# The same block kernel, with the instruction order of the scheduler's other simulation

## The chip, the cores and the metric

The kernel runs on one core of a Trainium2 chip. A core has engines that each work through a queue of their own, in order: PE (TensorE, matrix products; PEld is its weight load, which overlaps the products), DVE (VectorE), ACT (ScalarE), POOL (GpSimd) and SP (SyncE, which here issues the DMA transfers). An instruction starts when it is at the head of its queue and the semaphores that it waits for have been signalled. The metric is the device time of one execution in microseconds (us); less is better.

## The reference, cut to what matters

One decoder block on a sequence of 512 tokens with 1024 channels, in float32:

```python
mod = (silu(c) @ w_ada + b_ada)                       # six vectors: shift, scale, gate, twice
h = rmsnorm(x) * (1 + scale_m) + shift_m
z, xbc, dt_raw, u_pool, gate_logits = split(h @ w_in)
xs, bmat, cmat = split(silu(causal_conv4(xbc)))       # 2048, 4 x 128, 4 x 128 channels
dt = softplus(dt_raw + dt_bias);  a = -exp(a_log)     # 32 heads in 4 groups
y = ssd_chunked_scan(xs * dt, dt * a, bmat, cmat) + d_skip * xs     # chunks of 128 tokens
y_ssd = rmsnorm_per_group(y * silu(z)) @ w_branch_ssd
y_pool = causal_multiscale_pool(u_pool) @ w_branch_pool
x = x + gate_m * ((g_ssd * y_ssd + g_pool * y_pool) @ w_out)        # g_*: sigmoid(gate_logits)
h = rmsnorm(x) * (1 + scale_f) + shift_f
x = x + gate_f * (square(relu(h @ w_up)) @ w_down)    # 4096 inner channels
return rmsnorm(x)
```

In the scan, each chunk has a decay matrix exp(a_cs[l] - a_cs[s]) for l >= s, where a_cs is the cumulative sum of dt * a within the chunk, and a state that is carried from chunk to chunk.

## The kernel before, in words

Everything is kept with channels on the 128 partitions and the 512 tokens along the free axis. A float32 product is made of three products of a reduced-precision format: each operand is split in a high part (a cast on ACT) and a low part (a subtraction on DVE), and `mm3` issues high x high (L155), high x low (L156) and low x high (L157).

A *unit* is 128 output channels of a projection: `load_unit` loads a 128x1024 weight block by DMA (L140), casts its high part on ACT (L145) and makes its low part on DVE (L146); then 8 x 3 matmuls write one of three PSUM banks in rotation. What reads the bank frees it for the unit three later: the convolution (L395 on ACT, then three L397 on DVE), SiLU (L439, L412), a copy or an addition (L459, L461). Where an instruction that frees a bank stands late in its queue, the later unit waits on PE.

The stages are these. An opening, to about 58 us, in a `manual_schedule` block (first projections, L328). The dt chain: softplus by a series of small DVE operations (L355 to L367), cumulative sum as a matmul (L369), copy (L370), transposes (L373), two activations (L374, L375) and two stores to DRAM (L376 `cs_d`, L377 `ecs_d`). Then four groups of the scan. In a group, `prepare` broadcasts rows of `cs_d` from DRAM to all partitions (L494), adds and exponentiates small decay vectors (L496, L497, L498), masks on POOL (L499), exponentiates eight 128x128 blocks (L503) and multiplies by the scores (L504); transposes (L507) and products follow (L533 old state, L541 and L545 new state, L553 diagonal part), the sum (L561, L571, L573), the gate (L575), squares (L576) and their sums on POOL (L577, L578). At a group's end stands the split of the sums of squares (L125, L126), a matmul that adds them over partitions (L590), a logarithm and an exponential (L593, L594) and the scaling (L600). The function `run` writes units of the next projections between the steps of a group, so that PE has work. The modulation vectors come from `ada`: a 512 KB load (L170 `adaT`) and one DVE reduction (L171), also written between.

After the groups follow the pooling branch, the gates as pairs of half-width products with combined operands (`Pair`, splits at L691 and L692, products at L745), the output projection with residual (L933), squares and their sum (L940, L941), the norm's matmul L950 and its activations (L952, L953), and the scaled input of the MLP (L980 to L982). The MLP begins with four plain products at once (`up_first`) and four plain units, whose Relu, square and split (L1040, L1041, L691, L692) free the two banks they rotate over, and goes on in pairs.

The text of the program does not fix the order in the queues. Apart from the opening, the tile scheduler takes the instructions of the program, simulates the engines and puts out the order of each queue; `high_priority` and `issue_after` in the code are hints and constraints for it. The program gives it no table of numbers; how the simulation is made is a parameter of the context, at L1230. ACT keeps one set of function tables loaded at a time, and a table load is put in wherever neighbouring activations in the order belong to different sets.

## Time and profile before

| | before |
|---|---|
| time, 3 runs | 978.68, 978.77, 980.02 us; median 978.77 |
| the profiled execution | 978.15 us, of which the span from first to last instruction is 976.4 |
| busy: PE, DVE, ACT, POOL | 951.4, 689.7, 517.0, 90.8 us |
| mean granted clock of PE | 0.995 |
| DMA | 129.25 MB, 132 GB/s over the span |

PE is busy in 97% of the span, so time is lost wherever PE waits. The view of waits names for each wait of an engine the line that it waited for; the view of windows gives busy time by stretch; the timeline gives the instructions of one engine in order, with the idle time before one and what ended it in brackets. Consecutive instructions of one engine overlap by some 0.1 us in these rows, so spacings are a little shorter than durations.

### The profile page before, as it was taken

The page shows a single profiled execution, that of the slowest core. Times are in us where ns is not written, and L with a number is a line of the kernel's source. Part 1 is how long each engine was busy: PE and PEld are TensorE (multiplying, and loading weights), DVE is VectorE, ACT ScalarE, POOL GpSimd, SP SyncE. Part 2 cuts the span into 40 slices and gives each one's busy share as a digit, 9 for nine tenths or more (in the row PEclk, how much of TensorE's full clock was granted, in tenths as well). Part 3 has the DMA queues.
Part 4 walks back from the last instruction along what each step waited for, and adds up shares of the span by engine and source line. Part 5 has one row for each costly group of instructions (what it writes and reads, how often), then busy time and mean ns, then how long its engine had stood idle before and what let it go on. Part 6 is the DMA issues. An engine that isn't in the chain of part 4 may idle for free.

```text
span 976.4 us, 13664 instructions
## 1 busy us (share of the span) xinstructions
PE 951.4 (97%) x5279; PEld 810.0 (83%) x5279; DVE 689.7 (71%) x1025; ACT 517.0 (53%) x843; POOL 90.8 (9%) x91
## 2 busy tenths in 40 slices
PE   8999999999899999999999999799999999999996
PEld 4877887888688888877888988798899889889986
DVE  7978879776967787998633797785557655765633
ACT  5479978567346642673421554585147226525732
POOL 0102321320212132300000000000000000000000
PEclk9999999999999999999999999899999999999999
DMA  9736345853464344445221278252244125214002
GB/s 358 300 130 188 126 137 162 211 154 107 152 177 137 92 114 130 145 150 162 83 88 42 66 262 276 87 175 65 65 122 139 57 74 183 78 42 145 30 1 87
DMA packets 62339, 129.25 MB, mean 132 GB/s; under 512 B 4737, under 2 KB 29569, under 8 KB 62274
## 3 DMA queue, kind: packets, MB, share of 16 engines
q1 hardware_dynamic: 62272, 128.38, 41.8%
q8 instruction: 41, 0.67, 0.3%
q14 instruction: 24, 0.20, 0.1%
q10 hardware_dynamic: 2, 0.00, 0.0%
HBM read 126.13 MB, written 2.23 MB: 131 GB/s over the span
## 4 chain that ended last, share of the span: by engine, by line
PE 64%; DVE 16%; DMA 8%; ACT 7%; issue 3%; POOL 1%; SPq 0%; DVEq 0%; POOLq 0%; ACTq 0%
PE ps L156 15%; PE ps L157 15%; PE ps L155 15%; PE ps L745 14%; PE ps L328 4%; DMA d<-cs_d 4%; DVE d L146 3%; DVE s L126 2%; ACT d L145 2%; DMA d<-adaT 2%; DVE s L397 1%; DVE d L171 1%; DMA d<-wout 1%; DVE d L692 1%; ACT d L503 1%
## 5 line engine op out<-in xcount | busy, mean ns | idle before, releaser
L155 PE MATMUL ps<-s,d 128*128 128x512 f32 (+1 forms) x1016 | 386.8, 382 | 3.6 <-DVE s L397 2.9
L156 PE MATMUL ps<-s,d 128*128 128x512 f32 (+1 forms) x1016 | 383.4, 378 | 1.6 <-DVE s L126 1.6
L157 PE MATMUL ps<-s,d 128*128 128x512 f32 (+1 forms) x1016 | 383.7, 378 | 0.0
L155 PEld LDWEIGHTS ps<-s,d 128*128 128x128 f32 x1016 | 190.5, 188 | 42.7 <-issue 5.7
L156 PEld LDWEIGHTS ps<-s,d 128*128 128x128 f32 x1016 | 190.9, 188 | 36.7 <-DVE s L126 2.3
L157 PEld LDWEIGHTS ps<-s,d 128*128 128x128 f32 x1016 | 190.7, 188 | 35.7 <-issue 0.2
L146 DVE TENSOR_TENSOR d<-d,d 128x1024 fp32r<-128x1024 f32 x80 | 103.1, 1290 | 50.5 <-ACT d L145 25.6
L745 PE MATMUL ps<-s,d 128*128 128x256 f32 x1080 | 132.2, 280 | 0.0
L745 PEld LDWEIGHTS ps<-s,d 128*128 128x128 f32 x1080 | 129.9, 188 | 0.4
L145 ACT CAST d<-d 128x1024 fp32r<-128x1024 f32 x80 | 83.3, 1044 | 65.3 <-PE ps L157 20.9
L691 ACT CAST d<-d 128x1024 fp32r<-128x1024 f32 x56 | 58.3, 1050 | 99.1 <-PE ps L156 63.5
L692 DVE TENSOR_TENSOR d<-d,d 128x1024 fp32r<-128x1024 f32 x56 | 68.0, 1224 | 39.1 <-ACT d L691 23.3
L1121 DVE SCALAR_TENSOR_TENSOR xs<-ps,mod,xs 128x512 f32<-128x512 f32 x29 | 21.7, 750 | 69.6 <-PE ps L157 69.6
L691 ACT CAST d<-sz 128x1024 fp32r<-128x1024 f32 x32 | 33.6, 1051 | 68.8 <-PE ps L156 48.9
L171 DVE CUSTOM_DVE_ANT_0 d<-d,d,par_t 128x1024 f32<-128x1024 f32 x32 | 42.7, 1335 | 15.3 <-DMA d<-adaT 15.3
L692 DVE TENSOR_TENSOR d<-sz,d 128x1024 fp32r<-128x1024 f32 x32 | 39.2, 1224 | 19.7 <-ACT d L691 18.4
L503 ACT ACTIVATE d<-d,ncs 128x128 f32<-128x128 f32 x128 | 40.5, 391 | 6.7 <-POOL d L499 6.7
L328 PE MATMUL ps<-s,d 128*128 128x512 f32 x168 | 40.1, 392 | 1.9 <-ACT s L316 1.9
L397 DVE SCALAR_TENSOR_TENSOR s<-ps,par_t,s 128x511 f32<-128x511 f32 (+2 forms) x54 | 39.7, 742 | 0.2
L328 PEld LDWEIGHTS ps<-s,d 128*128 128x128 f32 x168 | 31.4, 188 | 9.6 <-ACT s L316 2.4
L125 ACT CAST s<-s 128x512 fp32r<-128x512 f32 x32 | 19.7, 618 | 25.4 <-POOL s L515 20.2
L126 DVE TENSOR_TENSOR s<-s,s 128x512 fp32r<-128x512 f32 x32 | 25.7, 803 | 9.2 <-ACT s L125 9.2
(230 smaller groups left out, 1098.5 us busy)
## 6 DMA issues: line engine op xcount, KB each, us to landing
d<-adaT SPq DMA_DIRECT2D x32, 512.0 KB, 4.1
d<-wx SPq DMA_DIRECT2D x18, 512.0 KB, 3.7
d<-wdn SPq DMA_DIRECT2D x18, 512.0 KB, 4.2
d<-cs_d SPq DMA_DIRECT2D x16, 512.0 KB, 6.2
d<-wbs SPq DMA_DIRECT2D x16, 512.0 KB, 3.8
d<-wz SPq DMA_DIRECT2D x15, 512.0 KB, 4.4
sz<-wdn SPq DMA_DIRECT2D x14, 512.0 KB, 3.8
d<-wup SPq DMA_DIRECT2D x13, 512.0 KB, 4.1
```

Of the source, the lines that this page charges most:

```text
L145: act.copy(hi[:, :w], r[:, a:a + w])
L146: (low or dve).tensor_tensor(lo[:, :w], r[:, a:a + w], hi[:, :w].bitcast(F32), ALU.subtract)
L155: pe.matmul(ps, whi, xhi[:, t0:t1], start=start, stop=False)
L156: pe.matmul(ps, whi, xlo[:, t0:t1], start=False, stop=False)
L157: pe.matmul(ps, wlo, xhi[:, t0:t1], start=False, stop=stop)
L171: dve.tensor_tensor_reduce(r, r, cbc, 1.0, col("b_ada", j), ALU.mult, ALU.add, mod[:, j:j + 1])
L328: pe.matmul(first[u], w[u][i // 2], h[k][i % 2], start=k == 0 and i == 0, stop=k == 7 and i == 2)
L397: dve.scalar_tensor_tensor(t[:, sh:], ps[:, :T - sh], w(3 - sh), t[:, sh:], ALU.mult, ALU.add)
L503: act.activation(m[:, i, :], m[:, i, :], AF.Exp, bias=ncs[:, c, g * HG + i:g * HG + i + 1])
L691: act.copy(dst[0], src)
L692: dve.tensor_tensor(dst[1], src, dst[0].bitcast(F32), ALU.subtract)
L745: pe.matmul(ps, x, y, start=start and m == 0 and i == 0, stop=m == 3 and i == 2, skip_group_check=True)
```

## The change

One argument of the scheduler's context:

```diff
-    with tile.TileContext(nc) as tc:
+    with tile.TileContext(nc, schedule_with_timeline_sim=True) as tc:
```

With it the scheduler makes its order with another simulation of the engines, one that follows the queues in time. The instructions of the block are the same, on the same engines and of the same sizes; activation-table loads fall from 40 to 29 because ACT's order is another, and the semaphore waits follow the order. Of PE's 5,000 instructions most stand elsewhere in the first 250 us (between a third and all of those in each 50 us from 50 us on, by up to some 150 places) and from 500 us on; from 250 to 450 us the order is nearly the old one. The opening is not moved.

Three places, as the prediction uses them. The first is DVE's queue at the end of the dt chain. `ncs` is the cumulative sum, `dec_80` a decay vector made from a broadcast, `s_100`, `s_103`, `s_150` and `s_163` are convolution tiles. Before:

```order
L366 SCALAR_TENSOR_TENSOR dtk<-s_90_514,dtk 128x128
L397 SCALAR_TENSOR_TENSOR s_100_570<-s_92_550,par_t,s_100_570 128x510
L367 TENSOR_TENSOR s_90_514<-dtk,ea 128x128
L397 SCALAR_TENSOR_TENSOR s_100_570<-s_92_550,par_t,s_100_570 128x509
L370 COPY ncs<-ps_31_178 128x128
L397 SCALAR_TENSOR_TENSOR s_103_578<-s_93_551,par_t,s_103_578 128x511
```

And in the change:

```order
L397 SCALAR_TENSOR_TENSOR s_140_803<-ps_139_778,par_t,s_140_803 128x509
L370 COPY ncs<-ps_31_178 128x128
L509 TENSOR_TENSOR s_154_894<-ps_153_889,dtk 128x512
L146 TENSOR_TENSOR d_191_1104<-d_189_1101,d_190_1103 128x1024
L146 TENSOR_TENSOR d_200_1168<-d_198_1165,d_199_1167 128x1024
L397 SCALAR_TENSOR_TENSOR s_150_864<-ps_149_839,par_t,s_150_864 128x511
L497 TENSOR_TENSOR dec_80<-d_124_712,ncs 128x8
L397 SCALAR_TENSOR_TENSOR s_163_934<-ps_162_909,par_t,s_163_934 128x511
L397 SCALAR_TENSOR_TENSOR s_150_864<-ps_149_839,par_t,s_150_864 128x510
L497 TENSOR_TENSOR dec_80<-d_130_742,ncs 128x8
L397 SCALAR_TENSOR_TENSOR s_163_934<-ps_162_909,par_t,s_163_934 128x510
L397 SCALAR_TENSOR_TENSOR s_150_864<-ps_149_839,par_t,s_150_864 128x509
```

The copy L370 stood among the convolutions of the first tiles; now it stands behind all of them and behind s_140's, and the two L497 that depend on it stand between the L397 of s_150 and s_163. In the order before, all L497 of this group stand behind the first convolutions and ahead of those of s_140.

The second is ACT's queue ahead of the first group's norm (L125 of `s_208`, whose result L590 multiplies). `sz_97` is the gated output of the group. Before:

```order
L576 ACTIVATE s_187_1087<-sz_97_561 128x512
L395 ACTIVATE s_193_1132<-ps_192_1107,par_t 128x512
L503 ACTIVATE d_244_1410<-d_244_1410,ncs 128x128 x8
L496 ACTIVATE cd_79<-d_268_1542 128x8
L576 ACTIVATE s_196_1151<-sz_97_561 128x512
L145 CAST d_239_1375<-d_238_1373 128x1024
L125 CAST s_208_1236<-s_123_711 128x512
```

And in the change:

```order
L576 ACTIVATE s_187_1087<-sz_97_561 128x512
L498 ACT_TABLE_LOAD
L498 ACTIVATE dec_81<-dec_81 128x8
L145 CAST d_261_1505<-d_260_1503 128x1024
L439 ACT_TABLE_LOAD
L439 ACTIVATE sz_178_1031<-ps_214_1251 128x512
L503 ACT_TABLE_LOAD
L503 ACTIVATE d_268_1542<-d_268_1542,ncs 128x128
L480 CAST s_227_1329<-ps_229_1331 128x384
L503 ACTIVATE d_268_1542<-d_268_1542,ncs 128x128
L576 ACTIVATE s_196_1151<-sz_97_561 128x512
L503 ACTIVATE d_268_1542<-d_268_1542,ncs 128x128 x6
```

The L125 of s_208 is the next row behind these. The work of the next group and its table loads now stand between the last squares and ahead of L125; further up, three more table loads stand between the square of s_168 and that of s_187.

The third is ACT's queue at the start of the MLP. `d_1064` is the high part of a weight block, `ps_1022` and `ps_1027` are banks of plain units. Before:

```order
L1040 ACTIVATE pad_1017_5828<-ps_978_5572 128x512
L1040 ACTIVATE pad_1018_5833<-ps_980_5574 128x512
L1041 ACTIVATE pad_1017_5828<-pad_1017_5828 128x512
L1041 ACTIVATE pad_1018_5833<-pad_1018_5833 128x512
L691 CAST s_1003_5804<-pad_1017_5828 128x512
L691 CAST s_1005_5806<-pad_1018_5833 128x512
L691 CAST pad_1089_6281<-pad_1082_6261 128x512
L1040 ACTIVATE pad_1023_5869<-ps_1022_5844 128x512
L691 CAST pad_1103_6361<-pad_1096_6341 128x512
L691 CAST d_1064_6104<-d_1063_6102 128x1024
L1041 ACTIVATE pad_1023_5869<-pad_1023_5869 128x512
```

And in the change:

```order
L691 CAST d_1064_6104<-d_1063_6102 128x1024
L1040 ACTIVATE pad_1017_5828<-ps_978_5572 128x512
L691 CAST pad_1103_6361<-pad_1096_6341 128x512
L1040 ACTIVATE pad_1018_5833<-ps_980_5574 128x512
L1041 ACTIVATE pad_1017_5828<-pad_1017_5828 128x512
L1041 ACTIVATE pad_1018_5833<-pad_1018_5833 128x512
L691 CAST s_1003_5804<-pad_1017_5828 128x512
L691 CAST s_1005_5806<-pad_1018_5833 128x512
L1040 ACTIVATE pad_1023_5869<-ps_1022_5844 128x512
```

The cast of d_1064 stood behind the Relu of ps_978, ps_980 and ps_1022; now it stands ahead of all three.

## The prediction

> **What bounds the kernel now.** I read the page first (engine shares), then PE's waits, then stretches of the places where the order changes, then the chain that ended last and the timelines there.
>
> ```profile
> span 976.4 us, 13664 instructions
> PE 951.4 (97%) x5279; PEld 810.0 (83%) x5279; DVE 689.7 (71%) x1025; ACT 517.0 (53%) x843; POOL 90.8 (9%) x91
> ```
>
> PE is busy 951.4 of 976.4 us, so every other engine together costs 25.0 us. An order that keeps PE's instructions can win 25 us at most; it can lose much more. Which waits make up the 25 us:
>
> ```profile
> PE ps L950 <- DVE sz L941: 5.1, 1, 5.1
> PE ps L156 <- DVE s L126: 3.1, 3, 1.5
> PE ps L155 <- DVE s L397: 2.9, 2, 2.5
> PE ps L328 <- ACT s L316: 1.9, 1, 1.9
> ```
>
> The one at L328 lies in the manually ordered opening, which the change leaves alone. Most of the rest is the start and the end of the program. Now the stretches (columns: length, PE, PEld, DVE, ACT, POOL busy, granted clock, DMA share, GB/s):
>
> ```profile
> 50.00:100.00 50.00, 49.23 (x242) 38.60 (x241) 39.83 (x68) 42.75 (x73) 8.36 (x8) 1.00 0.55 166
> 100.00:150.00 50.00, 50.00 (x271) 41.24 (x270) 40.84 (x65) 41.55 (x78) 14.40 (x14) 1.00 0.43 137
> 250.00:300.00 50.00, 47.10 (x265) 37.97 (x264) 38.95 (x63) 21.99 (x43) 10.62 (x12) 1.00 0.51 154
> 600.00:650.00 50.00, 44.93 (x351) 44.15 (x350) 39.20 (x83) 30.05 (x55) 0.00 (x0) 0.93 0.44 145
> 612.40:617.50 5.10, 0.05 (x1) 0.05 (x1) 4.03 (x7) 1.77 (x3) 0.00 (x0) 0.73 0.49 145
> 617.50:627.00 9.50, 9.50 (x62) 9.32 (x63) 7.27 (x19) 4.72 (x11) 0.00 (x0) 0.78 0.09 34
> ```
>
> From 50 to 150 us PE has 99.2 of 100 us of work, while DVE (39.8 and 40.8 of 50) and ACT (42.8 and 41.6) are busy some 80% and more. That stage has three almost full queues and little slack: it stays hidden behind PE only where each instruction comes in time. The last two rows show what an idle PE costs besides: after the 5.1-us wait the granted clock is below full, (1-0.73)x2x5.1 + (1-0.78)x2x9.5 = 6.9 us at half speed, of which 4.2 us under work. Half of that, 2.1 us, is lost on top.
>
> **The change part by part.** The instructions are the same, but for 11 activation-table loads fewer on ACT (40 to 29). That saving is work of an engine that is 47% idle; I price it at nothing for itself and count it inside the chains. All the rest is order. I followed the new queues by hand with the durations of the trace and list where PE would run into an operand that is not ready. Each term is (time of the longer chain) minus (time of PE's own work between the same two points).
>
> *A, the dt chain, +4.0.* The cumulative sum's copy L370 falls from between L397s of the first convolutions to behind them all. From the last L397 on, the masks depend on it: copy, transposes L373, L374, table load, L375, store to DRAM, broadcast L494, L497.
>
> ```profile
> 70.54 0.29 DVE L370 COPY ncs<-ps 128x128 f32<-128x128 f32 x1
> 71.41 1.22 DVE L146 TENSOR_TENSOR d<-d,d 128x1024 fp32r<-128x1024 f32 x1
> 80.75 0.74 DVE L397 SCALAR_TENSOR_TENSOR s<-s,par_t,s 128x509 f32<-128x509 f32 x1
> 82.99 0.17 DVE L497 TENSOR_TENSOR dec<-d,ncs 128x8 f32<-128x8 f32 x1 [1.42 <-DMA d<-cs_d]
> 85.23 0.17 DVE L497 TENSOR_TENSOR dec<-d,ncs 128x8 f32<-128x8 f32 x1 [2.08 <-DMA d<-cs_d]
> ...
> 26.59 4.78 PE ps L328 x21
> 74.75 6.42 DMA d<-cs_d
> ```
>
> Before, the second L497 comes 82.99-70.54 = 12.45 us after the copy, and only other work of DVE's own, already finished, stands near. Now an L397 of s_150, which must free the bank that the unit ps_182 takes, is queued behind two L497, and behind ps_182 all of PE is queued. Taking 0.4 off for transposes that start at the copy's end, the chain from the transposes is 12.05 + 0.17 + 2x0.66 (L397's spacing) = 13.5 us. PE's work between transposes and ps_182 is 36 matmuls of 4.78/21 = 0.228, 8.2, and 1.1 of small ones: 9.3. The difference is 4.2; I take 4.0. Bounds: 0 (a broadcast that lands 4 us earlier) and 6.2 (the third L497, which came 2.24 us after the second).
>
> *C, the first norm sum L590, +7.5.* It waits for ACT's L125 of s_208.
>
> ```profile
> L503 ACT ACT_TABLE_LOAD x8 | 10.3, 1283 | 0.1
> L576 ACT ACTIVATE s<-sz 128x512 f32<-128x512 f32 x16 | 10.1, 630 | 28.5 <-DVE sz L575 23.1 <-DVE pad L625 5.1
> L412 ACT ACTIVATE xs<-s 128x512 f32<-128x512 f32 x16 | 9.3, 624 | 0.0
> L439 ACT ACTIVATE sz<-ps 128x512 f32<-128x512 f32 x15 | 8.9, 595 | 0.1
> ...
> 125.75 2.45 ACT L503 ACTIVATE d<-d,ncs 128x128 f32<-128x128 f32 x8
> 136.80 1.04 ACT L145 CAST d<-d 128x1024 fp32r<-128x1024 f32 x1
> 132.57 0.62 ACT L125 CAST s<-s 128x512 fp32r<-128x512 f32 x1 [1.31 <-POOL s L578]
> ...
> 130.39 0.74 POOL L577 TENSOR_TENSOR s<-s 128x256 f32<-128x256 f32 x1 [3.16 <-ACT s L576]
> 131.22 1.32 POOL L578 TENSOR_TENSOR s<-s 128x128 f32<-128x128 f32 x1
> 130.62 1.60 DVE L171 CUSTOM_DVE_ANT_0 d<-d,d,par_t 128x1024 f32<-128x1024 f32 x1 [0.32 <-DMA d<-adaT]
> 126.13 4.47 DMA d<-adaT
> ```
>
> Between the exponent of dec_81 (L498) and the last square (L576) ACT's new queue holds six table loads (6 x 1.28 = 7.7), eight and two L503 (3.2), two casts (2.1), four 512-wide activations and one square (3.1) and small ones (1.3): 17.4, less some 0.7 of overlap, 16.7. POOL adds 2.1 and L125 0.6. In front of that L498 stand, on DVE, two ada reductions L171, each behind its adaT transfer (4.47): from the first one's landing to L497 1.6 + 1.3 + five L397 or L575-like of 0.66 + L146 1.2 + L561 1.1, about 9; the landing itself is some 9 us after L533 of ps_164. Sum from that L533: 9 + 9 + 16.7 + 2.1 + 0.6 = 37.5 to 38. PE has from there to L590 103 matmuls (23.5) and 7 of the SSD's small ones: 30.4. Difference 7.5. Bounds: 0 and 11 (the two transfers as slow as the broadcasts below).
>
> *E, F, G, second group, +3.8, +2.4, +2.3.*
>
> ```profile
> 162.49 6.15 DMA d<-cs_d
> 168.77 1.79 POOL d L499
> 184.43 8.02 DMA d<-cs_d
> ```
>
> On SP an adaT load whose slot must first be freed by DVE's L171 now stands ahead of the mask broadcast; then come 6.15 (landing), 1.79 (POOL), three L503 and a copy of 0.58, 9.5 in all, while PE has 25 matmuls (5.7) from the broadcast's issue to ps_279, which needs that copy's bank: 3.8. F is the same for ps_285 behind the 8.02-us broadcast; G is the state sum L545 behind two POOL masks. Bounds 0 and 14 for the three.
>
> *M, the start of the MLP, +5.7.* ACT's cast d_1064 moves ahead of the Relu of the first four products. It overwrites a buffer that PE reads in the last matmul of the unit ps_1027, and ps_1032, next on PE, waits for the Relu of ps_1022, behind it.
>
> ```profile
> 658.70 1.14 ACT L691 CAST s<-pad 128x512 fp32r<-128x512 f32 x2
> 659.73 0.63 ACT L691 CAST pad<-pad 128x512 fp32r<-128x512 f32 x1
> 660.25 0.60 ACT L1040 ACTIVATE pad<-ps 128x512 f32<-128x512 f32 x1
> 661.25 1.07 ACT L691 CAST d<-d 128x1024 fp32r<-128x1024 f32 x1
> ```
>
> While ACT works this off, PE has nothing: 1.07 for the cast, then seven 512-wide activations and casts at 0.5 each (two Relu, one weight part, two squares, two casts), and 0.60 for the last Relu: 5.2 to 5.7. The chain needs no transfer, so it is the surest term; bounds 4 and 7.
>
> *L, the removed wait, -5.1 and -2.1 of half clock.* L950 stands 21 matmuls (0.12 each, 2.5 us) later on PE, and SP issues the two wup blocks that hold DVE up two places earlier:
>
> ```profile
> 600.50 0.33 SPq L1019 DMA_DIRECT2D d<-wup  x1
> 604.14 0.33 SPq L1019 DMA_DIRECT2D d<-wup  x1
> ```
>
> 3.64 us earlier there and 2.5 us here exceed the wait of 5.1; bounds -2.5 and -7.2.
>
> *Small ones.* Six places where one or two instructions stand ahead of the one that frees PE's operand (first units, ps_164, the second L590, two in the MLP, the tail), each from 0.6 (a 512-wide activation) to 1.7 (one with a table load): +8.0 together, bounds 0 and 11. Of the old waits at L126, L397 and the 550 to 600 stretch, 2.0 go.
>
> *Q, half clock after the new waits, +6.* Each at 2.1, as above. The trace has a wait of 5.1 that brought it and one of 2.5 (within the 250 to 300 stretch, at clock 1.00) that did not. C and M are above 5.1; A and E lie between. I count three of the four: 6. Bounds 0 and 8.4.
>
> [...]
>
> Sum: 4.0 + 7.5 + 8.5 + 5.7 + 8.0 - 2.0 - 7.2 + 6 = 30.5 us. On the profiled execution, 978.15 us with 1.7 around its span, that is 1008.7; it lies 0.6 under the median of 978.77, so I say **1009 us**.
>
> **The rivals.** *Faster.* The new order fills PE's waits and the new chains do not decide, since broadcasts and adaT land early and ACT has 11 loads (14 us) less to do. Then up to 5.1 + 2.1 + 2.9 + 3.1 of the old waits go: 965. For it speaks that each term but M contains a transfer; against it that the broadcasts took 6.15 to 8.02 us. It decides only if the second L497 follows the transposes within PE's 9.3 us, and if M is wrong too. *No change.* Only A and M cost (9.7) and L and the lesser waits give it back (9.2): 979. It needs C to G hidden, that is ACT's queue of 16.7 us done in 10. *Slower, but less.* Waits that follow each other are not additive: what PE loses in A lets ACT and DVE catch up for C. With C, E, F and G at half, and Q at 4.2: 4.0 + 3.8 + 4.2 + 5.7 + 8.0 - 2.0 - 7.2 + 4.2 = 20.7, or 999. *Much slower.* The first stage becomes bound by DVE and ACT, each new broadcast queues as the 8.02-us one did, and every term is at its upper bound: 6.2 + 11 + 14 + 7 + 11 + 8.4 - 2.0 - 7.2 = 48, about 1027. *The order does not come out as listed*, because the device's queues sort it: I see no mechanism, since each engine's queue is in order.
>
> **How the numbers follow.** A difference below 0.2% (2 us) can't be told from none here. Forecast around 1009 (1003 to 1017): 0.45. Slower but less, 981 to 1003: 0.27. Much slower, above 1017: 0.16. No change: 0.05, faster: 0.07. The range from 987 to 1027 leaves out the last two cases, a part of the lesser loss and a little above. Chances: faster 0.07, same 0.05, slower 0.88.
>
> **What would show it.** In PE's waits: ps_182's L155 on DVE L397 near 4, L590 on ACT L125 near 7.5, L155 on ACT L459 twice, L155 on ACT L1040 of 5 to 6, and no L950 on L941. PE busy stays at 951 plus 2 per wait with half clock, and its clock row dips at the first and sixth of these, not at 615 us. ACT busy falls by 14. If PE's idle time stays near 25, the chains were wrong; if it grows in places that I do not list, the sum was right by luck.

## The result, and the profile after

| | before | the change |
|---|---|---|
| median (lowest to highest) | 979.39 us, 4 runs (978.68 to 980.11) | 1018.81 us, 4 runs (1016.29 to 1023.15) |
| the profiled execution, and its span | 978.15, 976.4 | 1016.84, 1015.1 |
| mean granted clock of PE | 0.995 | 0.981 |

The change is slower: the ratio is 1.0407, with a 95% interval from 1.0365 to 1.0449. The profiled executions differ by 38.7 us, and the page's first lines split them. They give busy time, share of the span and instructions of each engine:

```profile
span 1015.1 us, 13698 instructions
PE 964.2 (95%) x5279; PEld 814.9 (80%) x5279; DVE 690.9 (68%) x1025; ACT 518.5 (51%) x844; POOL 89.2 (9%) x91
```

PE's 5279 instructions are the same and take 12.8 us longer (964.2 against 951.4). PE's idle time has grown from 25.0 to 50.9, by 25.9. The view of waits of the change's PE says what the idle time waited for (in total, times, the longest):

```profile
PE ps L590 <- ACT s L125: 7.7, 2, 5.9
PE ps L155 <- ACT pad L1040: 6.7, 1, 6.7
PE ps L155 <- ACT s L459: 3.8, 2, 3.2
PE ps L155 <- DVE s L397: 3.7, 2, 3.6
PE ps L533 <- DVE s L545: 2.9, 1, 2.9
PE ps L155 <- ACT s L125: 2.1, 1, 2.1
PE ps L155 <- ACT s L691: 2.0, 2, 1.0
...
PE ps L155 <- ACT s L653: 1.8, 1, 1.8
PE ps L950 <- ACT s L1100: 1.7, 1, 1.7
PE ps L155 <- DVE s L461: 1.5, 1, 1.5
PE ps L156 <- DVE s L126: 1.3, 2, 1.1
```

Before, one wait stood out, L950 on L941 with 5.1. It is gone, and five others of 2.9 to 6.7 us, each at another place, have come, with some ten of 0.8 to 2.1. Most of the 12.8 us of extra busy time are the clock: in the stretches with a granted clock of 0.50 PE has 24.9 us of work in the change and 4.2 before, and by estimate half of the difference, some 10.3 us, is lost (behind the wait of 5.9 matmuls of L155 to L157 follow each other at 0.43 us, and ahead of it, at full clock, at 0.23). Of these 1.7 belong to a stretch at 14.8 us in the opening, which the change doesn't move. The other 2.5 us are busy time at full clock. Stretches of the change around two of the waits (length, PE busy, and so on as before; the number after POOL is the granted clock):

```profile
154.40:160.90 6.50, 0.64 (x3) 0.19 (x1) 2.44 (x4) 6.46 (x15) 1.18 (x2) 0.79 0.52 161
160.90:166.00 5.10, 5.06 (x14) 4.02 (x15) 5.08 (x5) 5.02 (x6) 0.00 (x0) 0.60 0.00 0
686.50:693.40 6.90, 0.26 (x2) 0.00 (x0) 5.21 (x9) 5.32 (x9) 0.00 (x0) 0.80 0.66 215
693.40:698.00 4.60, 4.58 (x12) 3.63 (x13) 1.93 (x3) 2.88 (x5) 0.00 (x0) 0.56 0.02 4
```

In the first row ACT is busy for 6.46 of 6.50 us while PE has nothing to do; behind each wait PE works at a clock of about 0.6, 12 to 14 matmuls in the time of some 20 at a spacing of 0.23 us.

Where in the program the time is lost is seen by comparing when PE has issued the same number of instructions. The change is later by 6 us at 100 us of the kernel before, 13 at 150, 21 at 200, 24 at 250, and still 24 at 300; by 31 at 460 and 32 at 600; by 25 at 622 (the wait at L950 is not there any more); by 34 at 665, and by 36 to 38 from 800 on. So 24 us are lost in the first two groups of the scan, 8 from the third group to 600 us, 9 at the start of the MLP and some 4 behind it, and 7 are won at L950.

### The profile page after: what moved, and what is told of

Same layout as the page of the kernel before. It is cut to its first block, busy times and chain, and to the rows that moved or that the text cites. A ratio compares the mean times of both kernels' runs of the same rounds, so it can differ in the third digit from the quotient of the medians.

```text
span 1015.1 us, 13698 instructions
## 1 busy us (share of the span) xinstructions
PE 964.2 (95%) x5279; PEld 814.9 (80%) x5279; DVE 690.9 (68%) x1025; ACT 518.5 (51%) x844; POOL 89.2 (9%) x91
## 4 chain that ended last, share of the span: by engine, by line
PE 74%; DVE 10%; DMA 6%; ACT 5%; issue 4%; POOL 1%; SPq 0%; DVEq 0%; POOLq 0%; ACTq 0%
PE ps L155 18%; PE ps L156 18%; PE ps L157 18%; PE ps L745 13%; PE ps L328 4%; DMA d<-cs_d 3%; PE ps L553 1%; DVE d L146 1%; DVE d L692 1%; DVE pad L635 1%; DMA d<-wout 1%; ACT d L503 1%; DVE d L171 1%; DVE s L126 1%; PE ps L533 1%
## 5 line engine op out<-in xcount | busy, mean ns | idle before, releaser
L155 PE MATMUL ps<-s,d 128*128 128x512 f32 (+1 forms) x1016 | 387.2, 387 | 24.5 <-ACT pad L1040 6.7
L157 PE MATMUL ps<-s,d 128*128 128x512 f32 (+1 forms) x1016 | 384.7, 381 | 0.0
L155 PEld LDWEIGHTS ps<-s,d 128*128 128x128 f32 x1016 | 191.7, 190 | 66.2 <-ACT pad L1040 7.1
L157 PEld LDWEIGHTS ps<-s,d 128*128 128x128 f32 x1016 | 192.2, 189 | 36.4 <-issue 0.3
L145 ACT CAST d<-d 128x1024 fp32r<-128x1024 f32 x80 | 83.6, 1046 | 101.5 <-PE ps L156 41.3
L146 DVE TENSOR_TENSOR d<-d,d 128x1024 fp32r<-128x1024 f32 x80 | 99.4, 1242 | 47.2 <-ACT d L145 21.2
L692 DVE TENSOR_TENSOR d<-d,d 128x1024 fp32r<-128x1024 f32 x56 | 68.0, 1223 | 39.8 <-ACT d L691 23.9
L692 DVE TENSOR_TENSOR d<-sz,d 128x1024 fp32r<-128x1024 f32 x32 | 39.1, 1224 | 22.8 <-ACT d L691 21.6
L328 PE MATMUL ps<-s,d 128*128 128x512 f32 x168 | 41.5, 402 | 1.9 <-ACT s L316 1.9
L328 PEld LDWEIGHTS ps<-s,d 128*128 128x128 f32 x168 | 32.6, 195 | 10.0 <-ACT s L316 2.4
L397 DVE SCALAR_TENSOR_TENSOR s<-ps,par_t,s 128x511 f32<-128x511 f32 (+2 forms) x54 | 39.4, 740 | 0.4 <-ACT s L395 0.2
L126 DVE TENSOR_TENSOR s<-s,s 128x512 fp32r<-128x512 f32 x32 | 25.8, 805 | 11.7 <-ACT s L125 11.4
L692 DVE TENSOR_TENSOR s<-pad,s 128x512 fp32r<-128x512 f32 x38 | 25.8, 686 | 10.5 <-ACT s L691 10.4
```

What stands on the lines that cost most here:

```text
L145: act.copy(hi[:, :w], r[:, a:a + w])
L146: (low or dve).tensor_tensor(lo[:, :w], r[:, a:a + w], hi[:, :w].bitcast(F32), ALU.subtract)
L155: pe.matmul(ps, whi, xhi[:, t0:t1], start=start, stop=False)
L157: pe.matmul(ps, wlo, xhi[:, t0:t1], start=False, stop=stop)
L328: pe.matmul(first[u], w[u][i // 2], h[k][i % 2], start=k == 0 and i == 0, stop=k == 7 and i == 2)
L397: dve.scalar_tensor_tensor(t[:, sh:], ps[:, :T - sh], w(3 - sh), t[:, sh:], ALU.mult, ALU.add)
```

## The experiments

All of them are the changed kernel with one added function, which chains each engine's instructions in a given order and adds no wait that the data don't ask for:

```diff
+def pin(tc, nc):
+    """Chain the instructions of each engine in the order of ORDER (issue order only, no waits)."""
...
+            tc.add_manual_dep(traced[b], a, info, reason="order")
...
         block_kernel(tc, out=out, **args)
+        pin(tc, nc)
```

ORDER is a list of instructions for each engine: the change's, the one before, or a join of both, cut at a time of the profile of before ("to 90 us": on each engine, what has started by then). So each run computes the whole block, and only the places in the queues differ. Ratios are against the kernel before on the same chip.

**The method itself.** ORDER is the change's own, with nothing moved.

> The changed kernel's own order, fixed by the same edges that the other runs use: 1016 to 1023 us, the same waits within 0.5 us each. It shows that fixing the order costs nothing, and gives a second profile of the same order. In the first profile half clock followed waits of 1.9, 2.1, 2.9, 3.2, 3.6, 5.9 and 6.7 us, but not waits of 1.5, 1.7, 1.8 and 1.8; the half-clock stretches begin and end on a grid of 3.41 us. If the clock falls when PE was idle for more than about 1.85 us of one interval of that grid, waits of 2 to 3.5 us get half clock in one profile and not in the other, by where the grid lies, while 5.9 and 6.7 get it in both; the times differ by 1.7 us for each.

It took 1021.10 us (1016.56 to 1023.94), ratio 1.0435 (1.0398 to 1.0472), against 1.0407 of the change. The same waits stand at the same places within some 0.6 us, but for L155 on L461, which is 2.9 instead of 1.5. What follows: fixing the order in this way changes the time by no more than the runs differ among themselves, and differences of 2 or 3 us between runs of this kind don't say much. That the order, and nothing else of the argument, makes the loss is shown by the run with before's order but for one stretch ("The part that gains"): it keeps the argument and takes 975.39 us.

**C, the first norm sum.** The two last squares are moved ahead of the table loads and L125 ahead of the next group's masks, on ACT (and its split's second half L126 on DVE ahead of an L146):

```diff
 L496 ACTIVATE cd_79<-d_268_1542 128x8
+L576 ACTIVATE s_187_1087<-sz_97_561 128x512
+L576 ACTIVATE s_196_1151<-sz_97_561 128x512
 L412 ACT_TABLE_LOAD
...
 L145 CAST d_261_1505<-d_260_1503 128x1024
+L125 CAST s_208_1236<-s_123_711 128x512
 L439 ACT_TABLE_LOAD
...
-L576 ACTIVATE s_196_1151<-sz_97_561 128x512
-L503 ACTIVATE d_268_1542<-d_268_1542,ncs 128x128 x6
-L125 CAST s_208_1236<-s_123_711 128x512
+L503 ACTIVATE d_268_1542<-d_268_1542,ncs 128x128 x7
```

> The order of the changed kernel, every queue fixed by issue-order edges, with five instructions moved at the first group's end: on ACT the squares L576 of s_187 and s_196 go ahead to behind L496 of d_268, the split L125 of s_208 to behind the cast L145 of d_261; on DVE L126 of s_209 goes ahead of L146 of d_262. The wait of L590 (5.9 us, and 2.0 us of half clock under work behind it) has nothing to wait for then. Theory A (each wait has its own price, as in my sum): 5.9 + 2.0 less, 1018.8 - 7.9 = 1011 us, and the waits behind it stay as they are. Theory B (in the first two groups ACT and DVE are behind, and a wait taken from one place comes back at the next instruction of PE that needs them): L590's wait falls below 1 us, but within the next 15 us of PE's work a new wait on L125 or L126 of the second group appears, or the 3.2 us at L459 grows, and the time falls by less than 3 us.

It took 1016.83 us (1015.55 to 1020.47), ratio 1.0386 (1.0354 to 1.0419): 2 us less than the change, inside both intervals. The wait of 5.9 at L590 is gone. In its place PE waits twice further on, as the timeline of this run shows, first PE's rows, then ACT's:

```profile
171.12 0.79 PE L155 MATMUL ps<-s,s 128*128 128x512 f32 x1 [4.49 <-ACT s L125]
176.76 0.79 PE L156 MATMUL ps<-s,s 128*128 128x512 f32 x1 [1.79 <-DVE s L126]
```

```profile
165.02 1.28 ACT L593 ACT_TABLE_LOAD   x1
...
167.02 1.28 ACT L594 ACT_TABLE_LOAD   x1
...
170.46 0.60 ACT L125 CAST s<-s 128x512 fp32r<-128x512 f32 x1
```

The work that L125 of s_208 was moved past (a SiLU and the masks, each with a table load) now runs behind it; then come the two loads for the norm, and the L125 of the next group that PE needs comes behind all of this. In this run ACT works from 142.68 to 173.15 without a gap. ACT is the limit of this stretch, so this edit in its queue chose which instruction of PE waits, and hardly how long PE waits in all (49.2 us idle in this run's profile, 50.9 in the change's).

**A, the dt chain.** First it is undone: the order of before to 90 us, the change's from there on.

```diff
-ORDER: the change's
+ORDER: before's to 90 us, then the change's for all that is left
```

> Every queue has the order of the kernel before for what starts there in its first 90 us (the whole dt chain, the first masks and all that stands between), and the order of the changed kernel for all the rest. Theory A: the waits of the first 90 us go, 1.0 at L385, 3.6 at L397 and 1.7 of half clock: about 6 us less, 1013 us, and L590 waits 6 to 7 us as before. Rival: the late dt chain, which leaves ACT idle for some 12 us between 88 and 102 us, is the root of all waits up to 210 us; then nearly all of the 24 us of that stage come back, 995 to 1000 us.

It took 1012.62 us (1012.33 to 1016.56), ratio 1.0347 (1.0316 to 1.0377), 6.2 less than the change. The waits at L397 (3.6) and L385 (1.2) are gone, those of the groups stand nearly as they were: L590 5.2, L459 3.6, and L461 even 3.0. What A's own waits and one stretch of half clock cost (3.6 + 1.2 + 1.7 = 6.5) is about what came back. So the late dt chain is not the root of the 24 us of the first groups; that rival falls. Then the opposite, A alone: the change's order to 102 us (its own time) and before's from there on.

```diff
-ORDER: the change's
+ORDER: the change's to 102 us, then before's for all that is left
```

> The change's order until 102 us (the dt chain late, the new first units) and before's order from there on. Undoing this part in the change took 6.2 us. Theory that each part has a price of its own, which can be added: 977 + 6 = 983, between 980 and 986. Rival, that the price depends on the order around it: before's groups have their broadcasts and convolutions placed for an early dt chain, so they meet a chain that is some 15 us late with several waits of 2 to 5 us between 100 and 130 us, and half clock after them: 994 to 1000.

It took 992.97 us (989.67 to 993.87), ratio 1.0145 (1.012 to 1.017): 14 us for the part whose removal gave 6. That is far from the sum (980 to 986) and just under the rival's range (994 to 1000). The waits of PE in this run, and then its chain of work that ended last at the first of them:

```profile
PE ps L156 <- DVE s L126: 6.6, 5, 3.1
PE ps L155 <- ACT s L125: 5.2, 2, 4.8
```

```profile
97.30 6.02 DMA d<-cs_d
...
104.83 2.44 ACT d L503 x8
107.27 0.51 ACT s L125
```

In before's order the eight masks and the splits of the first chunk stand directly behind the broadcast, for a chain that is early; when the broadcast comes late (landing at 103.32 here), they all wait for it, and PE behind them. The change's order has other work there. A part of an order has no price of its own here: the late chain costs 6 in the order made with it, and 14 in the one made without it. The waits lie right behind the join at 102 us, and no other cut was tried, so how much of the 14 belongs to this one join is not shown.

**M, the start of the MLP.** First the cast of d_1064 (and its DVE half L692) is put back behind the Relu of ps_1022, as my theory had it:

```diff
-L691 CAST d_1064_6104<-d_1063_6102 128x1024
 L1040 ACTIVATE pad_1017_5828<-ps_978_5572 128x512
...
 L1040 ACTIVATE pad_1023_5869<-ps_1022_5844 128x512
+L691 CAST d_1064_6104<-d_1063_6102 128x1024
```

> The order of the changed kernel, with the cast L691 of d_1064 (and its DVE half L692) moved back to behind the Relu L1040 of ps_1022, as the kernel before has it; the cast of pad_1103, which waits for a wup transfer, stays between the Relus of ps_978 and ps_980. If the cast makes the wait of 6.7 us before ps_1032, as I forecast, some 5 us of it and 2 us of half clock go: 1012 us. If the transfer behind pad_1103 decides, since everything behind it on ACT can't start before it lands, the wait shrinks by less than 1.5 us: 1017 to 1019 us.

It took 1021.76 us (1018.2 to 1022.38), ratio 1.0423 (1.0386 to 1.0459): nothing won, and the wait for L1040 is 6.9. My theory of M falls. The second run moves the cast of pad_1103 as well, which stands two rows further on:

```diff
-L691 CAST d_1064_6104<-d_1063_6102 128x1024
...
-L691 CAST pad_1103_6361<-pad_1096_6341 128x512
...
 L1040 ACTIVATE pad_1023_5869<-ps_1022_5844 128x512
+L691 CAST pad_1103_6361<-pad_1096_6341 128x512
+L691 CAST d_1064_6104<-d_1063_6102 128x1024
```

> As in the run with the cast moved back, and the cast L691 of pad_1103 (with its L692) moved back behind the same Relu too. Both stand as before; the Relus start when PE's products are done. The wait before ps_1032 falls from 6.7 to 2 to 3.7 us, by the five 0.5-us activations that still stand between the Relu of ps_978 and that of ps_1022, and the time by 3 to 6 us: 1013 to 1016 us. If even then 5 us or more are left, the cause lies ahead of these rows, in ACT's queue before the Relu of ps_978.

It took 1014.94 us (1013.38 to 1016.39), ratio 1.0361 (1.0333 to 1.0388), 3.9 less than the change, and the wait is 3.5, both as expected. The intervals of the two ratios overlap a little; the fall of the wait is the clearer sign. The third puts the whole start of the MLP in before's order, on all engines and the transfers too:

```diff
-ORDER: the change's
+ORDER: the change's to 660 us (its own time), before's to 680 (before's time), then the change's
```

> The change's order, but with before's between 660 and 680 us of before's time: the whole start of the MLP on all engines, the transfers' issues too. Moving the cast and the split of d_1064 alone took nothing, moving pad_1103's cast as well took 3.5. Theory that the start waits for ACT's queue ahead of the Relu of ps_1022, part of it held by a transfer: all of the wait goes, 6.7, and with it the half clock of 1.7: against the change 8 less, 1010, between 1007 and 1013. Rival, that the start is late because ACT and DVE come late out of the stage ahead: a wait of over 2 stays and the time is 1014 to 1018.

It took 1014.03 us (1011.25 to 1017.16), ratio 1.0367 (1.0339 to 1.0395), 4.8 less than the change by the medians and 3.9 by the ratios. A wait of 2.6 stays, so the rival, which gave 1014 to 1018, is right. The chain of this run at that wait:

```profile
679.94 1.19 DVE d L692
...
681.15 5.82 DMA d<-wdn
...
687.05 1.05 ACT d L691
...
691.55 0.61 ACT pad L1040
```

The weight load started at 681.15, when DVE's L692 (679.94 to 681.13) had freed its buffer. So 4.1 of the 6.7 us go with the order at the start of the MLP, and 2.6 stay, in this chain because DVE and the transfers come late out of the stage ahead. Why they are late there was not followed further.

**The halves.** Before's order to 253 us and then the change's; the change's to 277 us (its own time) and then before's:

```diff
-ORDER: the change's
+ORDER: before's to 253 us, then the change's
```

> Every queue has the order of the kernel before for what starts there in its first 253 us (opening, dt chain, the first group and most of the second), and the order of the changed kernel for all the rest. If the losses of the two parts are independent, this takes away the 24.2 us by which the changed kernel is late when it has issued the same number of products: 1018.8 - 24.2 = 994.6 us, 991 to 998. If the later part's waits come from lateness of the first part's, clearly less than 991; if the seam adds waits of its own, above 998.

```diff
-ORDER: the change's
+ORDER: the change's to 277 us, then before's
```

> The counterpart: every queue has the changed order for what starts there in its first 277 us, and the order of the kernel before for all the rest. Independent parts: 979.4 + 24.2 = 1003.6 us, 1000 to 1007, with the 5.1-us wait of L950 back. The two halves' differences to the kernel before add up to that of the whole change, 39.4, within 4 us.

The first took 1001.74 us (999.81 to 1007.54), ratio 1.0251 (1.0213 to 1.0289), 24.6 us over before; the second 998.73 (997.18 to 999.63), ratio 1.0205 (1.017 to 1.0241), 21.6 over. Together that is 46, more than the change's 39.4, so both forecasts were missed: the first run is above its 991 to 998, the second a little below its 1000 to 1007, with 3.6 us and not 5.1 at L950. The first run has a wait of 5.56 us right at its join, on an L397, where the kernel before has 2.48. Whether that belongs to the join was tried with a later cut:

```diff
-ORDER: before's to 253 us, then the change's
+ORDER: before's to 300 us, then the change's
```

> Before's order until 300 us of the block and the change's after that; the earlier run of this kind joined the two orders at 253 us and had a wait of 5.6 us and half clock right at the join. Theory that this wait belongs to the join: the wait near 261 is again 2.5 or less, and the rest costs what the change is later behind 300 us, about 15 (L1040 6.7, the second L590 1.8, L125 2.1, two L691 1.0, half clock 3.4 less the 5.1 of L950): 993, between 990 and 996. Rival, that the change's second half costs more once the first is on time (its 24.6 of that run): 1000 to 1003.

It took 995.49 us (994.44 to 996.43), ratio 1.018 (1.0155 to 1.0206), 16.4 us over before by the medians and 17.6 by the ratio, and the wait on L397 is 2.4 again. With it the halves add up to 21.6 + 16.4 = 38 of 39.4 us. Neither of the two runs has the change's order between 253 and 300 us of before, but there the change loses nothing (24 us late at 250 and at 300). So a little over half of the loss comes from the first 277 us, and what stands behind 300 us costs about the same whether or not the first part is late: some 15 us in the change, 16 to 18 here. The wait at the start of the MLP, too, is 6.3 us in this run.

**The part that gains.** Before's order, and the change's only between before's 540 and the change's 643 us, where L950 stands:

```diff
-ORDER: the change's
+ORDER: before's to 540 us, the change's to 643 (its own time), then before's
```

> The kernel before, except that between its 540 us (last gates) and the end of the output projection (623 us there, 643 us in the changed kernel) every queue has the changed order: the one place in which I forecast that the change wins. There L950 stands 21 products later and two wup blocks are issued two places earlier. If that order wins by itself, the wait of 5.1 us and 2.1 us of half clock go, and waits of some 1 to 2 us come in place of 1.4 us: 979.4 - 7.2 + 1 = 973 us, faster than both. If the wait went away in the changed kernel only because its DVE had caught up in the longer run, L950 waits here too and the time is 977 to 981.

It took 975.39 us (973.32 to 977.50, 12 runs) against 977.16 (17 runs), ratio 0.9978 (0.9961 to 0.9994). The wait at L950 is gone, and with it the half clock of the kernel before at 615 us, so this order does win by itself; some small waits have come (1.9 on L145, 1.0 on L777). This run's profile has half clock at 16.89 and at 262.65 instead (the section on the hardware comes back to both). So 1.8 us came of a wait of 5.1, less than the 6 of the forecast. Then single instructions were moved at the waits that were left, of which DVE's two largest are shown (the others are in the expectation):

```diff
+L397 SCALAR_TENSOR_TENSOR s_398_2270<-ps_397_2245,par_t,s_398_2270 128x511
+L397 SCALAR_TENSOR_TENSOR s_398_2270<-ps_397_2245,par_t,s_398_2270 128x510
+L397 SCALAR_TENSOR_TENSOR s_398_2270<-ps_397_2245,par_t,s_398_2270 128x509
 L146 TENSOR_TENSOR d_436_2481<-d_434_2478,d_435_2480 128x1024
...
+L126 TENSOR_TENSOR s_689_3806<-sz_464_2672,s_688_3805 128x512
+L600 SCALAR_TENSOR_TENSOR sz_464_2672<-sz_464_2672,par_t,s_687_3801 128x512
 L146 TENSOR_TENSOR d_725_4003<-d_723_4000,d_724_4002 128x1024
```

> The order of the splice (before's order, with the change's order only from before's 540 us to the change's 643 us), and five moves at the waits that are left: on DVE the three L397 of s_398 ahead of the weight split L146 of d_436 (the wait of 2.5 us at 261), L126 of s_237 ahead of L146 of d_284 (1.7 us at 160), L126 of s_689 and the fourth L600 ahead of L146 of d_725, on ACT L125 of s_694 ahead of an L846 (together some 2 us at 440), L692 of d_880 ahead of an L881 (0.6 us). Theory that single waits can be taken out where the instruction moved past is not needed by PE soon: the waits at 261, 160 and 440 fall from 2.4 + 1.7 + 2 to under 1.5 together, and no half clock after 261: 970, between 967 and 973. Rival, that each such move only hands the wait to the instruction that it is moved ahead of, as in the run at the group's end: the waits reappear within 20 us, 975 as the splice, plus or minus 1.5.

It took 975.80 us (973.98 to 978.24, 12 runs) against 979.06 (17 runs), ratio 0.9976 (0.9962 to 0.9989): as the run without the moves. Waits of PE, of the run without them and then of the run with them:

```profile
PE ps L156 <- DVE s L126: 3.8, 3, 1.7
PE ps L155 <- DVE s L397: 2.4, 1, 2.4
```

```profile
PE ps L156 <- DVE s L126: 3.4, 4, 1.4
PE ps L155 <- DVE s L397: 2.6, 4, 1.3
...
PE ps L590 <- DVE s L126: 1.0, 1, 1.0
```

One wait of 2.4 on L397 has become four with 2.6 together, and L590 waits 1.0 where it did not; PE is idle for 22.5 us in all, where it was 22.1. The rival of this run is right: the waits are handed on. Both joined orders are faster than the kernel before by 0.2%, each on a chip of its own, with an interval that ends below 1.

## Why the prediction was right or wrong

The time, 1018.8, lies in the range (987 to 1027) and on the side that had 0.88, but 10 us above the number and just above the likeliest case's own range (1003 to 1017). By its time it falls into "much slower" (above 1017, 0.16), and that case's first sentence, that the first stage becomes bound by ACT and DVE, fits what C's run shows of ACT; its sum of all upper bounds (48) did not come. On the profiled execution the sum said +30.5, and +38.7 came. Of the 30.5, 26.6 were waits and 3.9 half clock (6 for the new waits, less 2.1 for L950's). Measured are 25.9 of waits, some 10.3 of half clock and 2.5 of busy time at full clock. So the step that failed by its size is **Q**: it counts three waits that pay, and six did, for 10.7 us in place of 6, besides the 1.7 in the opening. It went by the trace's wait of 2.5, which did not pay, and that of 5.1, which did; here waits of 2.1 to 3.6 paid as well. That the total of the waits agrees so closely is in part luck, by the prediction's own sign: some 7 us of waits stand at places that it does not list (L125 at 468 us, L653, L461, L777, L145), and C, E and F are smaller than said by 4.

| term | predicted | measured |
|---|---|---|
| A, ps_182 on L397 | 4.0 | 3.6 |
| C, the first L590 on L125 | 7.5 | 5.9 |
| E and F, L155 on L459 | 6.2 | 3.8 |
| G, L533 on L545 | 2.3 | 2.9 |
| M, L155 on L1040 | 5.7 | 6.7 |
| L, L950 on L941 | -5.1 | -5.1 |
| old waits on L126, L397 | -2.0 | -4.6 |
| small ones (the rest) | 8.0 | 12.7 |
| half clock | 3.9 | 10.3 |
| busy time at full clock | 0 | 2.5 |

**A** came as worked out. The chain of work that ended last, of the change:

```profile
93.10 0.45 PE ps L373 x4
...
96.92 6.74 DMA d<-cs_d
103.67 0.60 DVE dec L497
104.27 1.32 DVE s L397 x2
105.73 0.47 PE ps L155
```

From the transposes to PE it takes 12.6 us, where 13.5 was said, and the broadcast is again more than half of it.

**C** has its mechanism and nearly its size. ACT's rows of the change, the table loads between the squares among them:

```profile
141.44 0.21 ACT L498 ACTIVATE dec<-dec 128x8 f32<-128x8 f32 x1 [1.48 <-DVE dec L497]
...
151.38 1.28 ACT L498 ACT_TABLE_LOAD   x1
...
153.84 1.28 ACT L439 ACT_TABLE_LOAD   x1
...
155.75 1.28 ACT L503 ACT_TABLE_LOAD   x1
...
158.01 0.62 ACT L576 ACTIVATE s<-sz 128x512 f32<-128x512 f32 x1
...
160.28 0.60 ACT L125 CAST s<-s 128x512 fp32r<-128x512 f32 x1
```

From L498 to the end of the last square ACT works for 17.2 us without a gap (16.7 was said), then come POOL, masks on ACT and L125 to 160.88. How the 1.6 us that are missing divide over the part ahead of L498, I can't tell from the rows. What the term did not say is that the wait has no price of its own here: with C undone, the time fell by 2, not by 5.9 and its half clock.

**M** had nearly its size for a wrong reason, which is luck. "The chain needs no transfer, so it is the surest term" is the sentence that failed. The chain of the change:

```profile
682.51 0.70 DVE s L692
...
683.22 6.11 DMA pad<-wup
689.36 0.62 ACT pad L691
...
692.05 0.70 DVE s L692
692.77 0.60 ACT pad L1040
693.42 0.80 PE ps L155
```

The cast in ACT's way is not d_1064's but pad_1103's, which waits for a weight transfer of 6.11 us; that transfer started when DVE's L692 had ended (683.21). I had read the order as a list of durations and not asked, for each row that moved, whether its own operand is there. Moving the one cast won nothing, both won 4, and the whole stage in before's order 4 to 5.

**E, F, G** stand where they were forecast, E (3.2 for 3.8) and above all F (0.6 for 2.4) smaller: the broadcast that ACT waits for ahead of F's copy took 6.21 us and not 8.02. **The small ones** were forecast by their kind (one or two instructions ahead of the one that frees an operand) and are half as much again. **L**'s wait went, though as part of the change that gave 7 and alone 1.8; whether PE's later place or the earlier loads did it was not separated.

**The table loads.** The text on the change and the prediction say that they fall from 40 to 29. That is wrong: the trace of the change has 41, that of the kernel before 40, and the profile page's ACT row says the same (844 instructions against 843, 518.5 us busy against 517.0). The forecast that ACT's busy time falls by 14 us was wrong with it, and the faster rival rested in part on it. The sum had priced it at nothing, so it does not move.

**The rivals.** "Slower, but less" was wrong in its time (999) and right in its sentence: waits that follow each other are not additive. It drew from that only that the sum is too large. The runs show both signs: undoing C gave less than its wait, the late chain alone cost more than its own.

## What to carry to other kernels

Where three engines are nearly full, price a new order stage by stage and not wait by wait: a wait that is taken out comes back at the instruction that was moved past, so a term worked out from one chain tells that the stage is late, not what undoing it gives. Follow every row that moves into a queue to its own operand, transfers and freed buffers included, before calling a chain free of them. And count half clock as a chance for every wait of about 2 us and more, not only for the longest: here those of 1.9 at L328 and of 2.5 on L397 were followed by it in one profile and not in another.

## What the runs showed of the hardware that was not expected

The half clock comes after much shorter waits than I had counted with. In the profiles of the kernel before and of the change its stretches last 3.41 us or 6.83 (except at the very end: 5.26 and 9.07), and their starts within one profile lie whole multiples of 3.41 us apart: 105 between the two of the kernel before, and 27, 15, 8, 7, 76, 65 and 93 between the eight of the change. The two rows of each fence are neighbouring intervals of such a grid. First the kernel before, then the joined order without the moves, which have almost the same wait on the same L397 (2.48 and 2.45 us; idle time is the length less PE's busy time):

```profile
259.80:263.21 3.41, 1.61 (x7) 1.38 (x8) 3.41 (x9) 1.58 (x3) 0.07 (x1) 1.00 0.88 286
263.21:266.62 3.41, 3.41 (x17) 2.80 (x16) 3.41 (x6) 1.91 (x2) 0.40 (x1) 1.00 0.37 111
```

```profile
259.24:262.65 3.41, 0.96 (x6) 0.67 (x4) 3.41 (x9) 0.78 (x2) 0.95 (x1) 1.00 0.86 243
262.65:266.06 3.41, 3.41 (x9) 2.65 (x9) 3.41 (x6) 2.71 (x3) 0.00 (x0) 0.50 0.68 213
```

In the first the wait lies across a border of the grid, 1.80 us of it idle in the interval, and the clock stays at 1.00. In the second 2.45 us fall into one interval and the next runs at 0.50, 9 matmuls in place of 17: by estimate half of the interval, 1.7 us, lost. In the profiles of the kernel before and of the change, the nine intervals at full clock with 1.90 to 3.41 us idle were all followed by half clock, and none with 1.75 or less was. Three lie between: one with 1.76 was (at 1004.66 us in the change), one with 1.76 (427.81, there too) and the 1.80 above were not. Once at half (the program's end aside), an interval with 2.66 to 2.79 us idle (614.79 before, 158.15 and 690.63 in the change) was followed by another at half, and one with 0.28 us idle (468.77 in the change) or none by full clock. In the change half clock came six times from the first group to the MLP, after the waits of 3.6, 5.9, 3.2, 2.9, 2.1 and 6.7 us, for 27 us at half clock under waits and work.

A little over half of an interval idle was enough here: 1.90 of 3.41 us, and once 1.76. Nor did the wait of 5.1 us of the kernel before have to fill one. In the two intervals of the grid around its start the clock falls after 2.41 us of idle time, in the middle of the wait:

```profile
611.38:614.79 3.41, 1.00 (x9) 0.80 (x7) 2.69 (x4) 1.96 (x3) 0.00 (x0) 1.00 0.13 24
614.79:618.20 3.41, 0.75 (x3) 0.66 (x3) 1.64 (x5) 0.83 (x2) 0.00 (x0) 0.50 0.78 256
```

So, by these profiles, whether the wait of 2.5 us on L397 paid some 1.7 us on top lay in where the grid fell in that execution. An order does not choose that: the wait of 1.9 us at L328 in the opening, whose order is the same in all these kernels, was followed by half clock in the change, where the 21 matmuls behind it took 6.66 us, and in three of the runs (6.65 in the joined order without the moves, 6.68 with them, 6.69 with A alone), and not in the kernel before (5.08) and in three others (5.05 to 5.07: the method itself, before's order to 300 us, the MLP's start in before's order). A forecast can give such a wait a chance of paying, and no more. The change's slowest run (1023.15) has a mean clock of 0.977 against 0.981 of the profiled one: 0.004 x 2 x 1020 = 8 us more at half clock, by estimate some 4 us lost of the 6.3 that lie between the two. It is not all of the spread: the run of 1020.78 has 0.981 as well.
